# Stick-breaking attention with queries on partitions, and sixteen weight sums in another stage

## The chip, the core and the metric

The kernel runs on one core of a Trainium2 chip. The metric is the device time of one execution, in microseconds (us), the median over the runs of a kernel. The engines are TensorE (PE in the profile, its weight loads PEld), VectorE (DVE), ScalarE (ACT), GpSimd (POOL) and SyncE (SP, which here only issues DMAs).

## The reference, cut to what matters

One step of a two-layer decoder for a prompt of 1024 tokens (two groups of 512) and 8 sample tokens that share all weights. Layer 0 has a gated recurrence and attention into 256 memory tokens, layer 1 has stick-breaking attention over shared keys and values and the same memory attention; each layer ends with a SwiGLU feed-forward network (FFN, width 2816). The change touches the prompt's stick-breaking attention, 4 heads of 128:

```python
z = jnp.einsum('bqhd,bkhd->bhqk', qi, kf) * scale + bf
mask = (k_pos[None, :] < pi[:, None])[None, None]
log_keep = jnp.where(mask, jax.nn.log_sigmoid(-z), 0.0)
tail = lax.cumsum(log_keep, axis=3, reverse=True) - log_keep
w = jnp.where(mask, jnp.exp(jax.nn.log_sigmoid(z) + tail), 0.0)
return jnp.einsum('bhqk,bkhd->bqhd', w, vf)
```

With softplus(z) = -log_sigmoid(-z), the exponent of a weight is z less the sum of the softplus values of this key and of all later keys that the query may see.

## The kernel before

**Staging.** Everything is float32. Projections use fp32r products of operands that are split in a high and a low part: ScalarE casts a weight tile to fp32r (L204, L489), VectorE subtracts it from the original (L205, L490), and three products are summed. A weight tile is loaded by SP's DMA queue; five raw tiles and five split tiles are there.

**Order.** A stage is a `weave` of generators: of the streams given with a number each, the one that has done the smallest share of its number takes its next step. A planner then orders each engine's instructions by what it expects to be ready, so that matmuls of one stream stand between those of another. Each engine works its queue in that order.

**The stages that matter.** At L1517 the attention of prompt group 0 (`b0.sb`, then `b0.mem`) is woven with the first parts of the FFN of layer 0, group 1, and with 16 steps of `weight_sums(1, ...)`. At L1520 come that FFN's other parts as `ffn_w`, with the other 24 sums. At L1534 the attention of group 1 is woven with the attention of the sample tokens (`sb_sample`, `mem_sample`) and the FFN of layer 1, group 0. From L1542 `ffn_w` runs once more, for layer 1, group 1.

**`ffn_w` and the sums.** This FFN form makes gate and up with seven products in place of eight (`gate_up_w`, L471). It needs sums of blocks of the gate and up weights; `weight_sums` (L538) makes them in DRAM, for each of five parts eight DMAs on GpSimd's queue, four of which add into their target. Ahead of each DMA stands a tiny copy on GpSimd (L551) that reads a tile which the FFN has just made, and so paces the sums. For the first few columns of the first part the plain form `gate_up_q` (L442) is used. Its products go to four single PSUM banks (`Q(0)` to `Q(3)`), which lie where the pairs of banks `mmp` of the stage before were. `S()` gives one of three other banks, `B()` one of seven 128 x 512 SBUF tiles.

**The attention before (`sb_prompt`, L1303).** Keys lie on partitions. For a head and a block of 128 keys, from the last block to the first: scores of the keys against all queries that may see them (L1319), bias and clamp on VectorE (L1324), softplus on ScalarE (L1297, L1298), on the diagonal a mask (L1301), a split in high and low (L225, L226). The sum over later keys is a product: a triangle (`trir`) times the split softplus adds to the bank `rr` (L1336), VectorE subtracts `rr` from the scores (L1341), and then the triangle's complement (`cmpr`) completes the block's column sums in `rr`. ScalarE takes the exponential (L1344), and the values times the weights add to the bank `po` (L1348). `rr` and `po` hold two of the three small banks for a whole head.

**The sample attention** of the same stage gathers its cached keys and values with an indirect DMA on GpSimd's queue (L953) into one of four tiles (`C()`), and VectorE multiplies them (L912, L924).

Of the kernel before, what the change touches and what calls it, by code (L numbers as in the profile page):

```python
# [10 lines left out]
F32R = mybir.dt.float32r  # L11
I32 = mybir.dt.int32
U8 = mybir.dt.uint8
AF = mybir.ActivationFunctionType
ALU = mybir.AluOpType
# [8 lines left out]
def tile_decoder(  # L24
# [63 lines left out]
    def B(dt=F32):  # L88
        return bpool.tile([P, 512], dt, tag="b", name=nm("b"))
# [5 lines left out]
    def Q(i):  # L95
        return single[0].tile([P, 512], F32, tag=f"q{i}", name=nm("q"))
# [24 lines left out]
    def S():  # L121
        return smp.tile([P, 512], F32, tag="s", name=nm("s"))
# [49 lines left out]
    def chain(*gens):  # L172
        for g_ in gens:
            yield from g_

    def weave(*streams):

        live = [[0, n, g_] for g_, n in streams]
        while live:
            cur = min(live, key=lambda e: e[0] / e[1])  # L180
            cur[0] += 1
            try:
                next(cur[2])
            except StopIteration:
                live.remove(cur)
# [38 lines left out]
    def split_to(dst, src):  # L224
        nc.scalar.copy(dst[0], src)  # L225
        nc.vector.tensor_sub(dst[1], src, dst[0].bitcast(F32))  # L226
# [212 lines left out]
            yield  # L439
        htok.append((ht, hs_))  # L440

    def gate_up_q(l, f, xt, side, n_side):  # L442

        h, n = PW[1], NG[1]
        sg = T()
        for j in range(2):
            w = split_w(w_gu[l], 0, ND, j * DFF + f * P)
            pp = [Q(2 * j + a) for a in range(2)]
            for k in range(ND):
                wh, wl = w[k]  # L450
                for wi, (wt, xi) in enumerate(((wh, 0), (wh, 1), (wl, 0))):
                    for a in range(2):
                        ins = nc.tensor.matmul(  # L453
                            pp[a][:, :h], wt, xt[k][:, xi, a * h : (a + 1) * h],
                            start=(k == 0 and wi == 0), stop=(k == ND - 1 and wi == 2),
                        )
                c = j * ND + k + 1
                for _ in range(c * n_side // 16 - (c - 1) * n_side // 16):
                    with tc.issue_after(ins.ins):
                        next(side, None)  # L460
            for a in range(2):
                d = sg[:, a * h : (a + 1) * h]
                if j == 0:
                    act[0] = nc.scalar.activation(d, pp[a][:, :h], AF.Silu)
                else:
                    nc.vector.tensor_mul(d, d, pp[a][:, :h])
        mt = M(F32R)
        split_to((mt[:, 0, :n], mt[:, 1, :n]), sg[:, :n])
        return mt
# [93 lines left out]
    class ffn_w:  # L563
# [38 lines left out]
        def part(self, pi):  # L602
            l, n, h = self.l, NG[1], PW[1]
            f0, nf = PARTS[pi]
            last = pi == len(PARTS) - 1
            mids = []
            for j in range(nf):
                self.pi = pi
                if f0 + j < self.plain:
                    mids.append(gate_up_q(l, f0 + j, self.x, self.sums, self.steps[j]))  # L610
                    now[0] = mids[-1][:, 0, 0:1].bitcast(F32)
                else:
                    mids.append(gate_up_w(l, f0 + j, self.ops, self.spl, self.raws))
                yield
            if pi == 0:
                self.R = R_one()
            if last:
                with tc.issue_after(act[0].ins):
                    nc.scalar.preload_act_table_set("natural_log_exp_and_others")
                if self.rows:  # L620
                    yield from self.close(f0, nf, mids)
                    return
                self.acc = small([P, WID], tag="st", bufs=3)
            for m in range(ND):
                w = split_w(w_down[l], f0, nf, m * P)
                pp = [Q(2 * (m % 2) + a) for a in range(2)]
                for k in range(nf):
                    wh, wl = w[k]
                    for wi, (wt, xi) in enumerate(((wh, 0), (wh, 1), (wl, 0))):
                        for a in range(2):  # L630
                            nc.tensor.matmul(  # L631
                                pp[a][:, :h], wt, mids[k][:, xi, a * h : (a + 1) * h],
                                start=(k == 0 and wi == 0), stop=(k == nf - 1 and wi == 2),
                            )
                for a in range(2):
                    d = self.R[m][:, a * h : (a + 1) * h]
                    if pi == 0:
                        nc.scalar.copy(d, pp[a][:, :h])
                    else:
                        nc.vector.tensor_add(d, d, pp[a][:, :h])  # L640
                now[0] = self.R[m][:, 0:1]
                if last:
                    sq_acc(self.acc, self.R[m][:, :n], m, n)
                if m % 2:
                    yield
# [649 lines left out]
    def softplus(zb, e, w):  # L1295

        nc.scalar.activation(e[:, :w], zb[:, :w], AF.Exp)  # L1297
        nc.scalar.activation(e[:, :w], e[:, :w], AF.Ln, bias=1.0)  # L1298

    def keep_strict(t):  # L1300
        nc.vector.tensor_mul(t, t, sm01)  # L1301

    def sb_prompt(g, Qs, xo):  # L1303
        nkb = CH * (g + 1)
        for h in range(H):
            kh, vh = A(), A()
            nc.sync.dma_start(kh[:, : g + 1, :G], ksc[h][:, : g + 1, :])
            nc.sync.dma_start(vh[:, : g + 1, :G], vsc[h][:, : g + 1, :])
            rr = S()
            po = S()  # L1310
            nc.vector.memset(rr, 0.0)
            nc.vector.memset(po, 0.0)
            for jb in range(nkb - 1, -1, -1):
                c0 = max(0, (jb - CH * g) * P)
                w = G - c0
                diag = jb >= CH * g
                kg, kc = jb // CH, (jb % CH) * P
                ps = S()
                nc.tensor.matmul(  # L1319
                    ps[:, :w], kh[:, kg, kc : kc + P], Qs[h // 2][:, h % 2, c0:G],  # L1320
                    start=True, stop=True,
                )
                zb = B()
                nc.vector.tensor_scalar(  # L1324
                    zb[:, :w], ps[:, :w], biasp[:, h : h + 1], 44.0, op0=ALU.add, op1=ALU.min
                )
                e = B()
                softplus(zb, e, w)
                if diag:
                    keep_strict(e[:, :P])  # L1330
                hi, lo = B(F32R), B(F32R)
                split_to((hi[:, :w], lo[:, :w]), e[:, :w])

                def acc(mat):
                    for s in (hi, lo):
                        nc.tensor.matmul(  # L1336
                            rr[:, c0:], mat, s[:, :w], start=False, stop=True, skip_group_check=True
                        )

                acc(trir)  # L1340
                nc.vector.tensor_sub(zb[:, :w], zb[:, :w], rr[:, c0:])  # L1341
                if jb:
                    acc(cmpr)
                nc.scalar.activation(zb[:, :w], zb[:, :w], AF.Exp)  # L1344
                if diag:
                    keep_strict(zb[:, :P])
                vt = vh[:, kg, kc : kc + P]
                nc.tensor.matmul(po[:, c0:], vt, zb[:, :w], start=False, stop=(jb == 0), skip_group_check=True)  # L1348
                yield
            d = xo[h]  # L1350
            split_to((d[:, 0, :G], d[:, 1, :G]), po)

# [68 lines left out]
    with tc.issue_after(made[0].ins):  # L1421
# [1 line left out]
        nc.gpsimd.affine_select(  # L1423
            trif, ones, pattern=[[-1, P]], compare_op=ALU.is_ge, fill=0.0, base=0, channel_multiplier=1
        )
        trir = const.tile([P, P], F32R, name="trir")
        nc.vector.tensor_copy(trir, trif)
        cmpr = const.tile([P, P], F32R, name="cmpr")
        nc.vector.tensor_sub(cmpr, ones, trif)

        sm01 = const.tile([P, P], F32, name="sm01")
        nc.gpsimd.affine_select(
            sm01, ones, pattern=[[1, P]], compare_op=ALU.is_gt, fill=0.0, base=0, channel_multiplier=-1
        )
        sel = const.tile([P, NB, NB], F32, name="sel")
        nc.gpsimd.affine_select(
# [77 lines left out]
    b0.open()  # L1514
    f1 = ffn(1, 0, o1.x)
    ws = weight_sums(1, range(5))
    weave((chain(b0.sb(), b0.mem()), 30), (chain(f1.part(0), f1.part(1)), 18), (islice(ws, 16), 17))  # L1517
    set_banks(True)
    fw = ffn_w(0, o1.x, (5, 6, 5), 2, False, f1.R)
    weave((chain(fw.part(2), fw.part(3), fw.part(4)), 24), (ws, 24))  # L1520
    f1.acc = fw.acc
    set_banks(False)
    xk1, xb1 = [], []
# [8 lines left out]
    b1.open()  # L1532
    f0 = ffn(0, 1, o0.x)
    weave(  # L1534
        (chain(b1.sb(), b1.mem()), 40), (chain(b1.sb_sample(), b1.mem_sample()), 39),
        (chain(f0.part(0), f0.part(1), f0.part(2), f0.part(3)), 34),
    )
    o1 = out_proj(1, 1, A, True)
    drain(o1.mm(b1.xo))
# [37 lines left out]
```

## Time and profile before

| | us |
|---|---|
| median of 3 runs | 2538.38 (2535.67 to 2547.71) |
| the profiled execution | 2532.34 |
| its span | 2530.6 |
| TensorE busy | 2489.4 |
| VectorE busy | 1599.8 |
| ScalarE busy | 1208.9 |
| GpSimd busy | 116.6 |

The profile is of one execution. A line such as L1336 names the line of the kernel, then engine, operation, the tile written and the tiles read. A matmul of full fp32 operands leaves two records, one of fp32r operands and a transpose leave one. The duration of one matmul includes its way through the array; matmuls overlap, so the time that one takes from the next is less than its duration, and is read from runs of equal matmuls. Waits are given with what ended them, for instance "PE s L1336 <- ACT b L225".

### The profile page before, as it was taken

The page shows a single profiled execution, that of the slowest core. Times are in us where ns is not written, and L with a number is a line of the kernel's source. Part 1 is how long each engine was busy: PE and PEld are TensorE (multiplying, and loading weights), DVE is VectorE, ACT ScalarE, POOL GpSimd, SP SyncE. Part 2 cuts the span into 40 slices and gives each one's busy share as a digit, 9 for nine tenths or more (in the row PEclk, how much of TensorE's full clock was granted, in tenths as well). Part 3 has the DMA queues.
Part 4 walks back from the last instruction along what each step waited for, and adds up shares of the span by engine and source line. Part 5 has one row for each costly group of instructions (what it writes and reads, how often), then busy time and mean ns, then how long its engine had stood idle before and what let it go on. Part 6 is the DMA issues. An engine that isn't in the chain of part 4 may idle for free. (4 is left out here: it accounts for less than half of the span.)

```text
span 2530.6 us, 40558 instructions
## 1 busy us (share of the span) xinstructions
PE 2489.4 (98%) x15295; PEld 2158.2 (85%) x15295; DVE 1599.8 (63%) x2926; ACT 1208.9 (48%) x2321; POOL 116.6 (5%) x187
## 2 busy tenths in 40 slices
PE   8999999999999999999999999999999999999998
PEld 6888888877877888999999989876676797999998
DVE  5766556655765576655645585666577638845666
ACT  5437543333434454555434454554454445554445
POOL 1000000000000000000011200011000000000000
PEclk9999999999999999999999999999999999999999
DMA  5355656555643446576789966544444333464552
GB/s 187 114 159 126 163 170 163 136 148 144 189 125 96 129 149 206 151 183 156 192 213 271 286 179 193 159 136 123 120 139 120 96 118 117 122 191 143 151 149 74
DMA packets 521551, 391.24 MB, mean 155 GB/s; under 512 B 19973, under 2 KB 459858, under 8 KB 521354
## 3 DMA queue, kind: packets, MB, share of 16 engines
q1 hardware_dynamic: 493194, 308.94, 41.2%
q0 software_dynamic: 28160, 79.70, 13.3%
q8 instruction: 120, 1.97, 0.3%
q14 instruction: 77, 0.63, 0.1%
HBM read 358.76 MB, written 101.11 MB: 182 GB/s over the span
## 5 line engine op out<-in xcount | busy, mean ns | idle before, releaser
L218 PE MATMUL mm<-x,ws 128*128 128x512 f32 (+1 forms) x6624 | 1235.4, 341 | 2.3 <-DVE t L235 1.4
L218 PEld LDWEIGHTS mm<-x,ws 128*128 128x128 f32 x6624 | 1017.2, 188 | 167.8 <-issue 25.3
L204 ACT CAST ws<-w 128x512 fp32r<-128x512 f32 (+1 forms) x672 | 395.7, 589 | 635.9 <-PE mm L218 479.3
L205 DVE TENSOR_TENSOR ws<-w,ws 128x512 fp32r<-128x512 f32 (+1 forms) x672 | 434.8, 651 | 288.3 <-ACT ws L204 276.5
L218 PE MATMUL mm<-m,ws 128*128 128x512 f32 (+1 forms) x1536 | 345.9, 372 | 0.2 <-DVE m L226 0.2
L218 PEld LDWEIGHTS mm<-m,ws 128*128 128x128 f32 x1536 | 257.4, 189 | 55.0 <-issue 9.5
L631 PE MATMUL q<-m,ws 128*128 128x260 f32 x1440 | 180.6, 286 | 6.6 <-DVE r L640 6.6
L631 PEld LDWEIGHTS q<-m,ws 128*128 128x128 f32 x1440 | 176.6, 191 | 9.1 <-DVE r L640 3.3
L490 DVE TENSOR_TENSOR ws<-w,ws 128x512 fp32r<-128x512 f32 x164 | 112.5, 691 | 84.5 <-ACT ws L489 82.4
L489 ACT CAST ws<-w 128x512 fp32r<-128x512 f32 x164 | 101.4, 621 | 105.6 <-PE q L631 34.3
L499 PE MATMUL q<-x,ws 128*128 128x260 f32 x1008 | 134.3, 282 | 0.0
L499 PEld LDWEIGHTS q<-x,ws 128*128 128x128 f32 x1008 | 126.4, 188 | 0.0
L499 PE MATMUL q<-y,ws 128*128 128x260 f32 x912 | 119.6, 283 | 0.4 <-ACT q L506 0.2
L499 PEld LDWEIGHTS q<-y,ws 128*128 128x128 f32 x912 | 113.6, 188 | 0.9 <-ACT q L506 0.4
L235 DVE TENSOR_SCALAR t<-mm 128x512 f32<-128x512 f32 (+1 forms) x70 | 48.4, 691 | 63.0 <-PE mm L218 62.8
L453 PE MATMUL q<-x,ws 128*128 128x260 f32 x576 | 72.6, 287 | 6.4 <-DVE r L390 5.3
L695 DVE TENSOR_TENSOR t<-t,mm 128x512 f32<-128x512 f32 (+1 forms) x54 | 37.2, 689 | 65.8 <-PE mm L218 65.8
L453 PEld LDWEIGHTS q<-x,ws 128*128 128x128 f32 x576 | 70.8, 192 | 8.2 <-ACT ws L204 3.9
L390 DVE TENSOR_TENSOR r<-r,mm 128x512 f32<-128x512 f32 (+1 forms) x72 | 49.4, 686 | 32.8 <-PE mm L218 31.9
L239 DVE TENSOR_TENSOR t<-t,t 128x512 f32<-128x512 f32 (+1 forms) x54 | 37.4, 692 | 51.4 <-ACT t L238 51.4
L226 DVE TENSOR_TENSOR m<-t,m 128x512 fp32r<-128x512 f32 (+1 forms) x88 | 60.9, 692 | 6.2 <-ACT m L225 5.1
L258 DVE TENSOR_TENSOR st<-st,n 128x512 f32<-128x512 f32 (+1 forms) x91 | 62.3, 691 | 3.4 <-ACT n L257 1.9
(343 smaller groups left out, 2859.3 us busy)
## 6 DMA issues: line engine op xcount, KB each, us to landing
w<-in_w_gu SPq DMA_DIRECT2D x310, 256.0 KB, 3.1
w<-in_w_down SPq DMA_DIRECT2D x160, 256.0 KB, 2.9
wsum<-in_w_gu POOLq DMA_DIRECT2D x36, 1024.0 KB, 9.5
w<-wsum SPq DMA_DIRECT2D x94, 256.0 KB, 3.2
w<-in_w_in_a SPq DMA_DIRECT2D x80, 256.0 KB, 3.1
w<-in_w_o SPq DMA_DIRECT2D x64, 256.0 KB, 2.9
wsum<-in_w_gu POOLq DMA_DIRECT2D x12, 1280.0 KB, 10.5
wsum<-wsum POOLq DMA_DIRECT2D x12, 1024.0 KB, 6.3
```

Of the source, the lines that this page charges most:

```text
L204: nc.scalar.copy(ws[:, 0, :n, :], raw[:, :n, :])
L205: nc.vector.tensor_sub(ws[:, 1, :n, :], raw[:, :n, :], ws[:, 0, :n, :].bitcast(F32))
L218: nc.tensor.matmul(ps[:, a, : PW[g]], wt, xt[k][:, xi, o : o + PW[g]], start=(k == 0 and wi == 0), stop=(k == nk - 1 and wi == 2),)
L226: nc.vector.tensor_sub(dst[1], src, dst[0].bitcast(F32))
L235: nc.vector.tensor_scalar(sv(x, g), pv(ps, g), -44.0, None, op0=ALU.max)
L258: nc.vector.tensor_add(acc[:, :n], acc[:, :n], t[:, :n])
L390: nc.vector.tensor_add(dst, dst, pv(ps, g))
L453: ins = nc.tensor.matmul(pp[a][:, :h], wt, xt[k][:, xi, a * h : (a + 1) * h], start=(k == 0 and wi == 0), stop=(k == ND - 1 and wi == 2),)
L489: nc.scalar.copy(w[:, 0, :], src)
L490: nc.vector.tensor_sub(w[:, 1, :], src, w[:, 0, :].bitcast(F32))
L499: nc.tensor.matmul(ps[:, :h], w[:, wj, k * P : (k + 1) * P], x[:, xi, :], start=(first and k == 0 and wi == 0), stop=(k == 3 and wi == 2), ...
L631: nc.tensor.matmul(pp[a][:, :h], wt, mids[k][:, xi, a * h : (a + 1) * h], start=(k == 0 and wi == 0), stop=(k == nf - 1 and wi == 2),)
```

## The change

Queries now lie on partitions and keys along the row. A unit is a block of 128 queries (`c`) against the keys of one group (`s`): its own group up to the diagonal (128 to 512 keys) or the whole earlier group (512). The first two widths of blocks 0 and 2 share a unit. The sum over later keys is a scan along the reversed row, `tensor_tensor_scan` with add, started for the earlier group from the last value of the later one. The weights are then transposed in blocks of 128 by TensorE, copied to SBUF by ScalarE, and multiplied with the values block by block. These last steps of a unit are issued after the first steps of the next unit. `trir`, `cmpr` and `rr` go, and the mask `sm01` is transposed.

Sixteen of the weight sums move from the weave at L1520 to that at L1534. The first product of the first plain `ffn_w` column goes to banks from `S()`. Three weave numbers change.

```diff
--- before.py
+++ after.py
@@ -439,13 +439,13 @@
             yield
         htok.append((ht, hs_))
 
-    def gate_up_q(l, f, xt, side, n_side):
+    def gate_up_q(l, f, xt, side, n_side, first):
 
         h, n = PW[1], NG[1]
         sg = T()
         for j in range(2):
             w = split_w(w_gu[l], 0, ND, j * DFF + f * P)
-            pp = [Q(2 * j + a) for a in range(2)]
+            pp = [Q(2 * j + a) if j or f != first else S() for a in range(2)]
             for k in range(ND):
                 wh, wl = w[k]
                 for wi, (wt, xi) in enumerate(((wh, 0), (wh, 1), (wl, 0))):
@@ -607,7 +607,7 @@
             for j in range(nf):
                 self.pi = pi
                 if f0 + j < self.plain:
-                    mids.append(gate_up_q(l, f0 + j, self.x, self.sums, self.steps[j]))
+                    mids.append(gate_up_q(l, f0 + j, self.x, self.sums, self.steps[j], PARTS[self.first][0]))
                     now[0] = mids[-1][:, 0, 0:1].bitcast(F32)
                 else:
                     mids.append(gate_up_w(l, f0 + j, self.ops, self.spl, self.raws))
@@ -1301,52 +1301,64 @@
         nc.vector.tensor_mul(t, t, sm01)
 
     def sb_prompt(g, Qs, xo):
-        nkb = CH * (g + 1)
+
+        units = [[(0, g), (2, g)], [(1, g)], [(3, g)]]
+        if g:
+            units = [u for c in ((0, 2), (1,), (3,)) for u in ([(i, 1) for i in c], *([(i, 0)] for i in c))]
+
+        def weights(h, kh, unit, first):
+            ps, spans, o = S(), [], 0
+            for c, s in unit:
+                w = (c + 1) * P if s == g else G
+                spans.append((c, s, o, w))
+                nc.tensor.matmul(
+                    ps[:, o : o + w], Qs[h // 2][:, h % 2, c * P : (c + 1) * P], kh[:, s, :w], start=True, stop=True
+                )
+                o += w
+            zb = B()
+            nc.vector.tensor_scalar(zb[:, :o], ps[:, :o], biasp[:, h : h + 1], 44.0, op0=ALU.add, op1=ALU.min)
+            e = B()
+            softplus(zb, e, o)
+            for c, s, a, w in spans:
+                if s == g:
+                    keep_strict(e[:, a + w - P : a + w])
+                d = e[:, a : a + w][:, ::-1]
+                nc.vector.tensor_tensor_scan(d, d, d, first.get(c, 0.0), op0=ALU.add, op1=ALU.max)
+                first[c] = e[:, a : a + 1]
+            nc.vector.tensor_sub(zb[:, :o], zb[:, :o], e[:, :o])
+            nc.scalar.activation(zb[:, :o], zb[:, :o], AF.Exp)
+            for c, s, a, w in spans:
+                if s == g:
+                    keep_strict(zb[:, a + w - P : a + w])
+            return zb, spans, o
+
+        def values(vh, po, zb, spans, n):
+            pt = S()
+            for o in range(0, n, P):
+                nc.tensor.transpose(pt[:, o : o + P], zb[:, o : o + P], ident)
+            wt = B()
+            nc.scalar.copy(wt[:, :n], pt[:, :n])
+            for c, s, a, w in spans:
+                for o in range(0, w, P):
+                    nc.tensor.matmul(
+                        po[:, c * P : (c + 1) * P], vh[:, s, o : o + P], wt[:, a + o : a + o + P],
+                        start=False, stop=(s == 0 and o == w - P), skip_group_check=True,
+                    )
+
         for h in range(H):
             kh, vh = A(), A()
             nc.sync.dma_start(kh[:, : g + 1, :G], ksc[h][:, : g + 1, :])
             nc.sync.dma_start(vh[:, : g + 1, :G], vsc[h][:, : g + 1, :])
-            rr = S()
             po = S()
-            nc.vector.memset(rr, 0.0)
             nc.vector.memset(po, 0.0)
-            for jb in range(nkb - 1, -1, -1):
-                c0 = max(0, (jb - CH * g) * P)
-                w = G - c0
-                diag = jb >= CH * g
-                kg, kc = jb // CH, (jb % CH) * P
-                ps = S()
-                nc.tensor.matmul(
-                    ps[:, :w], kh[:, kg, kc : kc + P], Qs[h // 2][:, h % 2, c0:G],
-                    start=True, stop=True,
-                )
-                zb = B()
-                nc.vector.tensor_scalar(
-                    zb[:, :w], ps[:, :w], biasp[:, h : h + 1], 44.0, op0=ALU.add, op1=ALU.min
-                )
-                e = B()
-                softplus(zb, e, w)
-                if diag:
-                    keep_strict(e[:, :P])
-                hi, lo = B(F32R), B(F32R)
-                split_to((hi[:, :w], lo[:, :w]), e[:, :w])
-
-                def acc(mat):
-                    for s in (hi, lo):
-                        nc.tensor.matmul(
-                            rr[:, c0:], mat, s[:, :w], start=False, stop=True, skip_group_check=True
-                        )
-
-                acc(trir)
-                nc.vector.tensor_sub(zb[:, :w], zb[:, :w], rr[:, c0:])
-                if jb:
-                    acc(cmpr)
-                nc.scalar.activation(zb[:, :w], zb[:, :w], AF.Exp)
-                if diag:
-                    keep_strict(zb[:, :P])
-                vt = vh[:, kg, kc : kc + P]
-                nc.tensor.matmul(po[:, c0:], vt, zb[:, :w], start=False, stop=(jb == 0), skip_group_check=True)
+            first, late = {}, None
+            for unit in units:
+                now_ = weights(h, kh, unit, first)
+                if late:
+                    values(vh, po, *late)
+                late = now_
                 yield
+            values(vh, po, *late)
             d = xo[h]
             split_to((d[:, 0, :G], d[:, 1, :G]), po)
 
@@ -1423,14 +1435,10 @@
         nc.gpsimd.affine_select(
             trif, ones, pattern=[[-1, P]], compare_op=ALU.is_ge, fill=0.0, base=0, channel_multiplier=1
         )
-        trir = const.tile([P, P], F32R, name="trir")
-        nc.vector.tensor_copy(trir, trif)
-        cmpr = const.tile([P, P], F32R, name="cmpr")
-        nc.vector.tensor_sub(cmpr, ones, trif)
 
         sm01 = const.tile([P, P], F32, name="sm01")
         nc.gpsimd.affine_select(
-            sm01, ones, pattern=[[1, P]], compare_op=ALU.is_gt, fill=0.0, base=0, channel_multiplier=-1
+            sm01, ones, pattern=[[-1, P]], compare_op=ALU.is_gt, fill=0.0, base=0, channel_multiplier=1
         )
         sel = const.tile([P, NB, NB], F32, name="sel")
         nc.gpsimd.affine_select(
@@ -1514,10 +1522,10 @@
     b0.open()
     f1 = ffn(1, 0, o1.x)
     ws = weight_sums(1, range(5))
-    weave((chain(b0.sb(), b0.mem()), 30), (chain(f1.part(0), f1.part(1)), 18), (islice(ws, 16), 17))
+    weave((chain(b0.sb(), b0.mem()), 25), (chain(f1.part(0), f1.part(1)), 18), (islice(ws, 16), 17))
     set_banks(True)
     fw = ffn_w(0, o1.x, (5, 6, 5), 2, False, f1.R)
-    weave((chain(fw.part(2), fw.part(3), fw.part(4)), 24), (ws, 24))
+    weave((chain(fw.part(2), fw.part(3), fw.part(4)), 24), (islice(ws, 8), 8))
     f1.acc = fw.acc
     set_banks(False)
     xk1, xb1 = [], []
@@ -1532,8 +1540,8 @@
     b1.open()
     f0 = ffn(0, 1, o0.x)
     weave(
-        (chain(b1.sb(), b1.mem()), 40), (chain(b1.sb_sample(), b1.mem_sample()), 39),
-        (chain(f0.part(0), f0.part(1), f0.part(2), f0.part(3)), 34),
+        (chain(b1.sb(), b1.mem()), 45), (chain(b1.sb_sample(), b1.mem_sample()), 39),
+        (chain(f0.part(0), f0.part(1), f0.part(2), f0.part(3)), 34), (ws, 17),
     )
     o1 = out_proj(1, 1, A, True)
     drain(o1.mm(b1.xo))
```

## The prediction

> **What bounds the kernel now.** I read the page first, then the busy time by stage, then TensorE's waits in each stage, then the DMA of the stages that lose time. The page's busy time by engine (us, share of the span, instructions):
>
> ```profile
> PE 2489.4 (98%) x15295; PEld 2158.2 (85%) x15295; DVE 1599.8 (63%) x2926; ACT 1208.9 (48%) x2321; POOL 116.6 (5%) x187
> ```
>
> TensorE is busy 98% of the span, so a matmul that goes is time that goes, unless a wait takes its place. Busy time is a share over the whole span, so the stages come next (columns: stretch, its length, busy time of each engine, granted clock, DMA share, GB/s).
>
> ```profile
> 915.00:1225.00 310.00, 309.82 (x2003) 275.47 (x2002) 187.25 (x347) 158.46 (x308) 15.36 (x28) 1.00 0.61 167
> 1225.00:1475.00 250.00, 238.72 (x1879) 233.28 (x1879) 144.35 (x286) 108.88 (x216) 40.95 (x60) 0.98 0.95 249
> 1600.00:2040.00 440.00, 434.55 (x1842) 317.04 (x1841) 292.76 (x485) 208.98 (x401) 25.43 (x24) 1.00 0.42 125
> 2150.00:2400.00 250.00, 247.49 (x2040) 244.20 (x2041) 157.60 (x310) 129.86 (x274) 0.00 (x0) 1.00 0.52 150
> ```
>
> These are the attention of group 0 (line 1517), the first Strassen FFN (line 1520), the attention of group 1 (lines 1534 to 1537), and most of the last FFN. TensorE idles 0.2, 11.3, 5.5 and 2.5 us in them. The two FFN stages do the same kind of work; the one that loses 11.3 us has the DMA engines 95% busy, the other 52%. TensorE's waits (us in total, times, longest) in the second, third and fourth stage:
>
> ```profile
> PE q L631 <- DVE r L640: 6.6, 5, 1.9
> PE q L453 <- DVE r L390: 3.7, 1, 3.7
> PE s L1336 <- ACT b L225: 2.1, 1, 2.1
> PE s L1336 <- DVE b L226: 1.9, 2, 1.0
> PE s L1348 <- DVE b L1301: 0.5, 2, 0.3
> PE q L453 <- DVE r L390: 1.5, 1, 1.5
> ```
>
> In the FFN, matmuls wait for VectorE to empty a bank (L640, L390). What keeps VectorE is seen from ScalarE's waits in that stage, and from the DMA rows (queue: packets, MB, share; transfers: count, KB, us to landing) there and, last two, in 2150 to 2400:
>
> ```profile
> ACT ws L489 <- DMA w<-wsum: 14.5, 3, 5.5
> ACT ws L204 <- DMA w<-in_w_down: 6.7, 1, 6.7
> q0 software_dynamic: 10924, 29.78, 48.9%
> w<-in_w_down SPq DMA_DIRECT2D x26, 256.0 KB, 5.7
> w<-wsum SPq DMA_DIRECT2D x18, 256.0 KB, 5.7
> w<-wsum SPq DMA_DIRECT2D x59, 256.0 KB, 3.2
> w<-in_w_down SPq DMA_DIRECT2D x24, 256.0 KB, 2.9
> ```
>
> So weights land late (5.7 us against about 3), ScalarE's cast of them waits, VectorE's split waits for the cast, and the evacuation queued behind the split holds TensorE. Half of the DMA engines' time there is GpSimd's queue, which is the weight sums. Each longer wait costs more than itself:
>
> ```profile
> 1254.30:1257.70 3.40, 2.93 (x13) 2.96 (x14) 2.21 (x5) 1.01 (x3) 0.00 (x0) 0.50 1.01 294
> ...
> 1715.10:1718.50 3.40, 3.40 (x10) 2.67 (x9) 2.67 (x8) 2.23 (x6) 1.96 (x2) 0.50 0.29 85
> ```
>
> These are the first and the last of four such rows (the others start at 1315.70 and 1452.30): after a wait the granted clock is 0.50 for 3.4 us, so 1.7 us are lost each time, three times in the FFN and once in group 1's attention.
>
> Here the Trainium skill ("TensorE: Matmul & The Clock Gate", section "HAM oscillation — how this bites in real kernels") speaks against counting all four: it asks for an idle gap of over about 3.4 us. By it one halving (after 3.7 us) hangs on these waits, and the sum below would gain 5.1 us less. The trace disagrees: the clock halved after waits of 1.9 and 2.1 us too.
>
> **The change part by part.** *Matmuls of the attention.* Gone are both products with the triangle and its complement (L1336). Rows: the two groups; then runs from the timeline (start, us), from which a price is the run less one duration, or the difference of two runs.
>
> ```profile
> L1336 PE MATMUL s<-b,trir x96: 222/394/800, 1028.4 to 1954.6; 128*128 128x512 f32 x48, 128*128 128x128 f32 x16, 128*128 128x256 f32 x16, 128*128 128x384 f32 x16
> L1336 PE MATMUL s<-b,cmpr x80: 222/342/825, 1029.5 to 1939.7; 128*128 128x512 f32 x32, 128*128 128x128 f32 x16, 128*128 128x256 f32 x16, 128*128 128x384 f32 x16
> 2135.64 13.31 PE L218 MATMUL mm<-m,ws 128*128 128x512 f32 x57
> 2037.34 22.84 PE L218 MATMUL mm<-x,ws 128*128 128x260 f32 x186
> L1319 PE MATMUL s<-a,a 128*128 128x512 f32 x48 | 25.1, 605 | 0.2 <-DVE b L1324 0.2
> 1769.66 1.02 PE L1319 MATMUL s<-a,a 128*128 128x512 f32 x2
> 83.97 1.06 PE L1130 MATMUL s<-a,a 128*128 128x128 f32 x8
> 85.30 1.95 PE L1130 MATMUL s<-a,a 128*128 128x128 f32 x16
> 2505.78 1.03 PE L732 MATMUL s<-ident,r 128*128 128x128 f32 x8
> 2520.01 1.47 PE L732 MATMUL s<-ident,r 128*128 128x128 f32 x12
> L218 PEld LDWEIGHTS mm<-x,ws 128*128 128x128 f32 x6624 | 1017.2, 188 | 167.8 <-issue 25.3
> ```
>
> An fp32r pass costs 13.31/57 = 234 ns at 512 columns and 22.84/186, about 122, at 260; 384 columns I put at 175 between them, 256 at 118, 128 at the 111 of the next price. Gone: 80 x 0.234 + 32 x (0.175 + 0.118 + 0.111) = 31.6 us. A full fp32 product is two records; one costs 1.02 - 0.605 = 0.42 us at 512 columns, 0.89/8 = 111 ns at 128, between them 0.32 at 384 and 0.21 at 256. A transpose is one record of 0.44/4 = 110 ns.
>
> Scores keep their columns (1280 a head in group 0, 3328 in group 1; only the operands swap roles): nothing. The weighted values were 48 x 0.42 + 16 x (0.32 + 0.21 + 0.11) = 30.4 us and become 36 blocks x 4 heads x 2 = 288 records of 128 columns, 32.0 us: +1.6. New are 144 transposes: +15.8. Net -31.6 + 1.6 + 15.8 = **-14.2 us**. The bound on the other side is the weight load, 188 ns by the last row if nothing hid it (a rival).
>
> Here the Trainium skill ("TensorE: Matmul & The Clock Gate", section "Back-to-back issue gap") gives about 81 ns a matmul at 128 columns with its weight load. By it the 432 new records would cost 13 us less than I count. The trace has 110 and 111, and I stay with it.
>
> *VectorE and ScalarE.* Rows by shape (count | busy, mean ns | idle before):
>
> ```profile
> L226 DVE TENSOR_TENSOR b<-b,b 128x512 fp32r<-128x512 f32 x24 | 16.6, 690 | 15.4 <-ACT b L225 15.4
> L1160 DVE COPY_PREDICATED b<-mask,s 128x256 f32<-128x256 uint8 x56 | 25.8, 527 | 0.0
> ```
>
> The split's subtraction goes; the scan comes over the same 18432 columns. No scan is in this trace. Bounds: a subtraction's 1.35 ns a column (25 us in all) and the dearest row a column, 2.06 ns (38 us); I take the upper end, as a scan feeds each result into the next. VectorE is free 123 us in the first attention stage and 147 in the second, so it costs nothing; without that cover it would cost the 13 us difference. Masks stay 64; the cast to hi is replaced by the copy of the transposed weights, of the same width. The clearing of rr and two constants go: nothing, VectorE isn't late there. Nor do the new shares of the weave: the attention keeps its pace in group 0 (20 steps at 25 for 24 at 30) and ends earlier in group 1, with FFN steps left to fill TensorE.
>
> *Waits in the chain.* Two of the three places where TensorE stood in an attention step go: the 4.0 us before L1336, also the 0.5 before L1348 and one halving of 1.7: 6.2. What is late next: transposes behind the exponential (one step later in the program, so a step of FFN matmuls lies between) and values behind ScalarE's copy. The memory attention has this very pattern, and its waits in 1600 to 2040 were:
>
> ```profile
> PE s L885 <- ACT b L883: 0.3, 1, 0.3
> ```
>
> In 40 units (3 a head in group 0, 7 in group 1) that is little; bounds 0 and 28 us (0.69 us each, a pass over 512 columns by L226's row).
>
> *Sixteen sums moved* out of the FFN at 1225. All that they issue goes with them: a mark on GpSimd and a transfer each of 512 x 512 x 4 bytes, 16 of that queue's 29.8 MB. That takes 0.49 x 16/29.8 = 0.26 off the DMA share, to 0.69. SP's queue, which loads the weights, keeps its transfers. The stage should then resemble its twin: of 11.3 us of idling and 5.1 of halved clock, 16.4 in all, I keep 3.4 (its twin's 2.5 and something for the eight sums left): **-13.0**. Bounds 0 and 16.4. They now run beside group 1's attention, where DMA goes from 0.42 to 0.42 + 0.26 x 250/440 = 0.57; at 0.61 the stage from 915 lost 0.2 us. Their first use is in the last FFN (line 1542). But GpSimd's queue also holds that stage's page gathers, and those have little cover:
>
> ```profile
> 1771.11 0.95 POOL L953 DMA_INDIRECT c<-in_cache_sb_v,pidx  x1 [0.30 <-issue]
> 1774.75 1.23 DVE L924 TENSOR_TENSOR c<-c,sc 128x1024 f32<-128x1024 f32 x1 [1.26 <-DMA c<-in_cache_sb_v,pidx]
> c<-in_cache_sb_v,pidx POOLq DMA_INDIRECT x16, 4.1
> c<-in_cache_sb_k,pidx POOLq DMA_INDIRECT x8, 10.1
> 1282.67 0.64 POOL L551 COPY mk<-m 128x1 f32<-128x1 f32 x1 [12.10 <-ACT m L225]
> ```
>
> VectorE already waited 1.3 us for a gather; beside the sums of 1225 to 1475 gathers landed in 10.1 us instead of 4.1, and a mark holds the queue until an FFN step is done (12.1 us here). Queued behind the waiting gather are VectorE's weight splits, and TensorE waits for these once the five buffers of split weights are used. I charge 3.8: the stage's waits net **-2.4** (6.2 - 3.8).
>
> *First bank of the FFN* taken from the small pool: the 1.5 us at 2150 go, **-1.5**; the 3.7 at 1254 are in the 13.0, since the weights were late there too.
>
> Sum: 14.2 + 13.0 + 2.4 + 1.5 = 31.1 us. The profiled execution took 2532.3 us (span 2530.6), so it becomes 2501.2. The median of the runs shown is 6.0 above that execution; I carry that over: **2507 us**, with 2494 to 2520 as this case's own range.
>
> **The rivals.** *The FFN keeps its stalls* (the change doesn't do what it says: its own weight loads, not the sums, fill the DMA). For it: eight sums stay. Against: the twin stage. Gives 2507 + 13 = 2520. *Weight loads bind the small passes*: 432 x 0.188 - 31.6 - 30.4 = +19.2 instead of -14.2, so 2540; against it the 111 ns of whole runs. *Values wait for the copies* at every unit: +28, 2535; against it the pattern's one wait of 0.3. *Slower: gathers behind sums.* In 1700 to 1780 eight tiles of cached values each come 6.0 us later (10.1 - 4.1), VectorE's queue stands, TensorE runs out of weights, and a halving of 1.7 follows: 8 x 7.7 = 62, 2569. It decides from 5.5 us lost a tile. For it: the 1.3 us already seen. Against: split weights lie ready, and sums are spread over 440 us. Two smaller cases lie within the forecast's own range and share its chance: the clock halves as often as now although waits go (4 x 1.7 back, 2514; 0.05), and small passes cost less than the 110 ns that every run of them shows (each 10 ns is 4.3 us; at 81 ns 2494; 0.03).
>
> **How the numbers follow.** Forecast 0.62, FFN stalls stay 0.12, copies 0.11, weight loads 0.05, gathers 0.07, others 0.03. About 0.5% (12.7 us) is what a measurement can tell from no change. Faster than 2525.7: the first two and a third of the others, 0.75. Within: copies, loads and a third of the others, 0.17. Slower: gathers and the rest, 0.08. The range goes down to 2492: every wait gone (3.4 + 3.8 less) gives 2500, without the 6.0 carried over 2494, and a little for the prices read from runs. It goes up to 2536, which takes in the stalls that stay and the copies. Loads, gathers, the others beyond it and the forecast's own tails are the 0.2 left out.
>
> **What would show it.** Per step: no L1336, 144 transposes at about 110 ns and 288 value passes at 111; 1225 to 1475 with DMA near 0.69, weights landing in under 4 us, no L631 wait over 1 us and no halved clock; the scan under 2.1 ns a column and VectorE under 75% in the attention; gathers landing in under 6 us there, and no VectorE wait on them over 3 us. Wrong if TensorE idles over 8 us in either attention stage, or if the FFN still waits on L640.

## The result and the profile after

| | us |
|---|---|
| before, median of 4 runs | 2537.03 (2531.45 to 2547.71) |
| changed, median of 4 runs | 2514.22 (2512.76 to 2514.93) |
| ratio of the medians, 95% interval | 0.9909 [0.989, 0.9928] |
| profiled execution, before and after | 2532.34 and 2513.78 |

The kernel is 23 us faster, where 30 were forecast. One term of the sum, group 1's attention, went the other way, and the stages show it. TensorE's busy time on the page of the changed kernel, then its stages (stretch, length, busy time of each engine, granted clock, DMA share, GB/s); group 1's attention starts 18 us earlier than before:

```profile
PE 2467.7 (98%) x15455; PEld 2160.5 (86%) x15455; DVE 1609.2 (64%) x2900; ACT 1197.4 (48%) x2289; POOL 119.6 (5%) x187
```

```profile
915.00:1225.00 310.00, 308.62 (x2071) 277.61 (x2070) 194.01 (x350) 158.83 (x303) 15.18 (x28) 1.00 0.62 168
1225.00:1470.00 245.00, 241.90 (x1900) 236.12 (x1900) 153.05 (x293) 114.03 (x221) 25.15 (x28) 0.99 0.71 195
1590.00:2030.00 440.00, 422.24 (x1960) 323.02 (x1959) 297.88 (x470) 199.97 (x384) 45.09 (x56) 0.98 0.57 160
2130.00:2400.00 270.00, 267.39 (x2203) 263.95 (x2201) 172.45 (x336) 144.12 (x301) 0.00 (x0) 1.00 0.53 152
```

The FFN idles 3.1 us instead of 11.3, with DMA at 0.71. Group 1's attention idles 17.8 us instead of 5.5, with DMA at 0.57 instead of 0.42. What TensorE waits for there, and VectorE's waits for DMA in the same stretch (us in total, times, longest):

```profile
PE s L1343 <- ACT b L1340: 5.1, 2, 3.9
PE s L1338 <- DVE b L1301: 5.0, 3, 4.5
PE s L878 <- DVE b L871: 4.4, 2, 2.5
PE s L1314 <- DVE b L1319: 2.5, 1, 2.5
```

```profile
DVE c L912 <- DMA b<-qd: 13.8, 9, 3.2
DVE c L924 <- DMA c<-in_cache_sb_v,pidx: 12.0, 2, 8.1
DVE c L924 <- DMA c<-in_cache_mem_v: 8.1, 5, 3.6
```

The waits stand at many lines, but the second list is one story: VectorE stands still 33.9 us for data of the sample attention (`qd` is the broadcast of the sample queries); before, these three rows were

```profile
DVE c L912 <- DMA b<-qd: 7.0, 5, 2.3
DVE c L924 <- DMA c<-in_cache_sb_v,pidx: 2.3, 3, 1.3
DVE c L924 <- DMA c<-in_cache_mem_v: 2.2, 2, 2.0
```

One case in order of time, from the timelines of GpSimd, VectorE and TensorE (start, duration, line, idle before):

```profile
1744.15 0.97 POOL L953 DMA_INDIRECT c<-in_cache_sb_v,pidx  x1 [17.20 <-PE ns L926]
1745.46 1.14 POOL L554 DMA_DIRECT2D wsum<-in_w_gu  x1
1746.90 1.05 POOL L953 DMA_INDIRECT c<-in_cache_sb_v,pidx  x1 [0.31 <-issue]
1756.42 1.23 DVE L924 TENSOR_TENSOR c<-c,sc 128x1024 f32<-128x1024 f32 x1 [8.11 <-DMA c<-in_cache_sb_v,pidx]
1762.69 1.09 PE L1338 MATMUL s<-ident,b 128*128 128x128 f32 x4 [4.47 <-DVE b L1301]
```

A tile of cached values comes in two gathers, and a sum of 1 MB was issued between them. The first gather landed in 4.0 us, the second in 9.4:

```profile
c<-in_cache_sb_v,pidx POOLq DMA_INDIRECT x1, 4.0
c<-in_cache_sb_v,pidx POOLq DMA_INDIRECT x1, 9.4
```

VectorE waits 8.1 us for the second one, the masks and scans queued behind come late, and TensorE stands 4.5 us at a transpose. Most gathers were not late: the median of the 16 is 4.6 us to landing, 4.1 before, and VectorE's 12.0 us are two waits, both for a gather issued behind a sum. Followed back in the same way on the timelines, TensorE's waits of 2.5, 4.5 and 1.2 us (at 1727, 1763 and 1768) stand behind these two gathers, and those of 3.9, 2.5 and 2.0 (at 1698, 1921 and 1930) behind the broadcast of the sample queries: about half of the 17.8 us each.

The clock is halved in three stretches of this stage instead of one, the first of twice the length; each begins within 1.3 us of the end of one of these waits (3.9, 2.5 and 4.5 us):

```profile
1697.40:1704.20 6.80, 6.46 (x22) 5.77 (x23) 4.61 (x11) 1.75 (x7) 0.95 (x1) 0.51 0.52 156
1728.10:1731.50 3.40, 3.40 (x14) 3.04 (x14) 3.33 (x5) 2.14 (x4) 0.00 (x0) 0.51 0.89 282
1762.20:1765.70 3.50, 3.01 (x7) 1.01 (x8) 2.48 (x7) 2.50 (x5) 0.00 (x0) 0.52 0.46 129
```

### The profile page after: what moved, and what is told of

The parts are those of the page before. It is cut to its first block, busy times and chain, and to the rows that moved or that the text cites. A ratio compares the mean times of both kernels' runs of the same rounds, so it can differ in the third digit from the quotient of the medians.

```text
span 2511.9 us, 40889 instructions
## 1 busy us (share of the span) xinstructions
PE 2467.7 (98%) x15455; PEld 2160.5 (86%) x15455; DVE 1609.2 (64%) x2900; ACT 1197.4 (48%) x2289; POOL 119.6 (5%) x187
## 4 chain that ended last, share of the span: by engine, by line
PE 90%; DVE 4%; DMA 3%; ACT 1%; issue 1%; SPq 0%; POOL 0%; DVEq 0%; ACTq 0%
PE mm L218 53%; PE q L499 11%; PE q L631 7%; PE q L453 2%; PE s L1150 2%; PE mm L1018 2%; DMA b<-qd 1%; PE s L1343 1%; PE s L885 1%; PE s L854 1%; PE mm L803 1%; PE mm L830 1%; PE s L1314 1%; PE q L663 1%; PE ns L926 1%
## 5 line engine op out<-in xcount | busy, mean ns | idle before, releaser
L218 PE MATMUL mm<-x,ws 128*128 128x512 f32 (+1 forms) x6624 | 1216.0, 340 | 2.4 <-DVE t L235 1.5
L218 PEld LDWEIGHTS mm<-x,ws 128*128 128x128 f32 x6624 | 1013.6, 189 | 155.5 <-issue 17.4
L218 PE MATMUL mm<-m,ws 128*128 128x512 f32 (+1 forms) x1536 | 329.3, 367 | 0.0
L499 PE MATMUL q<-x,ws 128*128 128x260 f32 x1008 | 134.3, 282 | 0.0
L499 PEld LDWEIGHTS q<-x,ws 128*128 128x128 f32 x1008 | 126.4, 188 | 0.0
L225 ACT CAST m<-t 128x512 fp32r<-128x512 f32 (+1 forms) x88 | 54.9, 624 | 21.7 <-DVE t L695 13.0
L453 PE MATMUL q<-x,ws 128*128 128x260 f32 x480 | 61.0, 288 | 3.7 <-DVE r L390 2.2
```

What stands on the lines that cost most here:

```text
L218: nc.tensor.matmul(ps[:, a, : PW[g]], wt, xt[k][:, xi, o : o + PW[g]], start=(k == 0 and wi == 0), stop=(k == nk - 1 and wi == 2),)
L453: ins = nc.tensor.matmul(pp[a][:, :h], wt, xt[k][:, xi, a * h : (a + 1) * h], start=(k == 0 and wi == 0), stop=(k == ND - 1 and wi == 2),)
L499: nc.tensor.matmul(ps[:, :h], w[:, wj, k * P : (k + 1) * P], x[:, xi, :], start=(first and k == 0 and wi == 0), stop=(k == 3 and wi == 2), ...
```

## The experiments

Two theories were set against each other. Late transfers: loads of the sample attention that share the DMA engines with the moved sums stop VectorE. The attention itself: the longer scan, and copies queued behind softplus on ScalarE, make the waits. The first four kernels:

**Sums back in the FFN** (`e1_sums_back`)

```diff
-    weave((chain(fw.part(2), fw.part(3), fw.part(4)), 24), (islice(ws, 8), 8))
+    weave((chain(fw.part(2), fw.part(3), fw.part(4)), 24), (ws, 24))
...
-        (chain(f0.part(0), f0.part(1), f0.part(2), f0.part(3)), 34), (ws, 17),
+        (chain(f0.part(0), f0.part(1), f0.part(2), f0.part(3)), 34),
```

> The changed kernel with the sixteen sums back in the FFN stage (line 1525 of the changed kernel), all else as changed. Late-transfer theory (gathers and loads queued beside the sums stop VectorE in group 1's attention): TensorE idles under 6 us in 1590 to 2030 (17.8 with the change), VectorE waits for cached values under 4 us in total (12.0), while the FFN stage idles about 11 us again with its clock halved two or three times; 2514 - 17 + 13 = about 2510 us. Attention theory (the new form itself, its longer scan and the copies queued behind ScalarE's softplus, makes the waits): the stage still idles 14 us or more, and the FFN's loss comes on top: about 2527 us.

Measured: 2514.8 us, ratio 0.9918 [0.9902, 0.9935]. Its FFN stage and group 1's attention:

```profile
1225.00:1470.00 245.00, 231.67 (x1824) 227.19 (x1824) 135.87 (x266) 103.96 (x204) 43.83 (x60) 0.97 0.95 249
1590.00:2030.00 440.00, 434.05 (x2097) 336.39 (x2097) 310.41 (x489) 208.49 (x397) 25.71 (x24) 1.00 0.42 127
```

The attention idles 6.0 us in place of 17.8 (5.5 before), the FFN 13.3 in place of 3.1. So the new attention by itself idles no more than the old one, and in the changed kernel the move of the sums paid nothing: what the FFN gained, the attention lost. The time is nearer to the 2510 of the late-transfer theory than to 2527. Its bound for cached values was too low: VectorE still waits 5.4 us for them, not under 4.

**The move alone, on the kernel before** (`e2_move_only`)

```diff
-    weave((chain(fw.part(2), fw.part(3), fw.part(4)), 24), (ws, 24))
+    weave((chain(fw.part(2), fw.part(3), fw.part(4)), 24), (islice(ws, 8), 8))
...
-        (chain(f0.part(0), f0.part(1), f0.part(2), f0.part(3)), 34),
+        (chain(f0.part(0), f0.part(1), f0.part(2), f0.part(3)), 34), (ws, 17),
```

> The kernel before with the sixteen sums moved to group 1's attention and nothing else changed. Late-transfer theory: the FFN stage gains about 11 us, group 1's attention loses 12 to 18 (it idled 5.5 us): 2532 to 2538 us, no gain. Attention theory: the FFN's gain remains, the old attention still idles about 5.5 us: about 2521 us.

Measured: 2545.4 us, ratio 1.0034 [1.0023, 1.0046]: 9 us slower, more than either theory said. Group 1's attention idles 21.7 us (5.5 before), the FFN 4.7 (11.3 before). The stage, TensorE's longest waits there, then one wait of VectorE for the broadcast and TensorE's wait behind it, from the timeline:

```profile
1600.00:2040.00 440.00, 418.29 (x1667) 299.48 (x1666) 281.81 (x468) 199.15 (x380) 46.38 (x56) 0.98 0.56 154
PE s L1336 <- ACT b L225: 14.9, 3, 6.9
```

```profile
1707.49 1.23 DVE L912 TENSOR_TENSOR c<-c,b 128x1024 f32<-128x1024 f32 x1 [7.07 <-DMA b<-qd]
1709.41 0.58 PE L1336 MATMUL s<-b,trir 128*128 128x256 f32 x1 [6.95 <-ACT b L225]
```

The broadcast comes through SP's queue, not GpSimd's, so the queue of gathers is not the only way in which the sums hurt. The old attention stands up to 7 us where VectorE stands. Its products with the triangle wait for the split on ScalarE and VectorE in the middle of each step; that this makes it lose more than the new form is argued, not shown.

**The FFN's first bank as before** (`e3_old_bank`)

```diff
-            pp = [Q(2 * j + a) if j or f != first else S() for a in range(2)]
+            pp = [Q(2 * j + a) for a in range(2)]
```

> The changed kernel with the first FFN product back in the bank that the stage before empties. If the small pool's bank was worth what the prediction said: the wait of L453 for L390 comes back at the last FFN (1.5 us) and grows at the first (2.2 us to about 3.7), so 2 to 3 us more than the changed kernel, 2517. If the weights were late anyway: within 1 us of it.

Measured: 2519.1 us, ratio 0.9929 [0.9912, 0.9945]. The two waits in its FFN stages, then the one in the changed kernel:

```profile
PE q L453 <- DVE r L390: 7.4, 1, 7.4
PE q L453 <- DVE r L390: 1.5, 1, 1.5
```

```profile
PE q L453 <- DVE r L390: 2.2, 1, 2.2
```

By the waits the bank is worth the 1.5 us in the last FFN and 5.2 in the first, more than the forecast gave it. The two kernels differ by 4.8 us, but the intervals of their ratios still overlap a little (0.9912 against 0.9928).

**Sums beside an earlier stage** (`e4_sums_early`)

```diff
-    weave((chain(a1.merge(), a1.mem()), 12), (a1.mem_sample(), 20), (chain(f0.part(2), f0.part(3)), 16))
+    early = weight_sums(1, range(3, 5))
+    weave(
+        (chain(a1.merge(), a1.mem()), 12), (a1.mem_sample(), 20), (chain(f0.part(2), f0.part(3)), 16), (early, 17),
+    )
...
-    ws = weight_sums(1, range(5))
+    ws = weight_sums(1, range(3))
```

and the weave of group 1's attention has no sums.

> The changed kernel with the sixteen sums in the weave of 700 to 850 us (DMA share 0.36, no page gathers) instead of group 1's attention. Late-transfer theory: the FFN keeps its gain and group 1's attention idles under 6 us: 2514 - 17 = about 2497 us. Attention theory: 2511 to 2515 us.

Measured: 2499.8 us, ratio 0.9863 [0.9847, 0.9879], faster than both kernels. The stage that took the sums, the FFN and group 1's attention:

```profile
700.00:850.00 150.00, 147.81 (x632) 110.63 (x631) 89.00 (x150) 59.07 (x120) 14.75 (x22) 1.00 0.72 192
1225.00:1470.00 245.00, 241.35 (x1909) 235.41 (x1908) 153.24 (x295) 114.03 (x223) 25.16 (x28) 1.00 0.72 196
1590.00:2030.00 440.00, 434.80 (x2115) 337.25 (x2114) 304.23 (x480) 207.25 (x396) 26.25 (x24) 1.00 0.42 127
```

The FFN keeps its gain (3.7 us of idling), the attention idles 5.2 us, and the stage that took the sums loses 2.2. The late-transfer theory stands; the time is 3 us above its 2497. VectorE's waits for cached values are 5.8 us here, which is what the stage has without any sums. What this left open: the marks or the transfers, the gathers' queue or the shared DMA engines, and whether VectorE had room at all.

**Sums in the second half of group 1's attention** (`e5_sums_late`; `pause(n, g)` yields n times, then runs `g`)

```diff
-        (chain(f0.part(0), f0.part(1), f0.part(2), f0.part(3)), 34), (ws, 17),
+        (chain(f0.part(0), f0.part(1), f0.part(2), f0.part(3)), 34), (pause(18, ws), 35),
```

> The changed kernel with the sixteen sums still in group 1's attention, but held back until half of the FFN steps there are done, after the last gather of cached values. Queue theory (what hurts are page gathers behind a sum in GpSimd's queue): VectorE's 12 us of waits for cached values go, the stage idles about 8 us, 2503 us. Bandwidth theory (any load that shares the DMA engines with a 1 MB sum lands late, also SP's broadcasts of the sample queries and its loads of the memory's values): the waits move to these, the stage idles 12 us or more, 2508 us or more.

Measured: 2502.1 us, ratio 0.9876 [0.9858, 0.9894]. VectorE's waits for DMA in the stage:

```profile
DVE c L917 <- DMA b<-qd: 8.8, 8, 3.6
DVE c L929 <- DMA c<-in_cache_mem_v: 5.8, 3, 3.1
DVE c L929 <- DMA c<-in_cache_sb_v,pidx: 4.8, 4, 2.6
```

Cached values are waited for 4.8 us instead of 12.0, the others still 14.6 (8.5 with the early sums). The stage idles 7.8 us (432.24 busy of 440), as the queue theory said. So most of the loss came from sums in the half with the gathers. The waits that SP's loads still cause cost TensorE 2.9 us in the second half. The run doesn't part the two causes: in the half that is now free of sums the broadcasts come nearer to their time too (2.5 us of waits up to 1740, 7.7 in the changed kernel).

**Marks alone** (`e7_marks_only`): the early sums, and in group 1's attention a stream of 16 copies as of L551, without a DMA.

> The kernel with the early sums, plus sixteen marks alone (the tiny copies on GpSimd that wait for the FFN) in group 1's attention, without transfers. If it is the marks that hold the gathers in GpSimd's queue: VectorE waits 10 us or more for cached values again, 2507 or more. If it is the transfers: within 2 us of the kernel with the early sums, 2498 to 2502.

Measured: 2501.3 us, ratio 0.987 [0.9849, 0.9891]; the stage idles 6.0 us (434.00 of 440), the waits for cached values are 6.1 us, against 5.8 without marks. Not the marks: the transfers.

**Every scan twice** (`e6_scan_twice`, on the early sums)

```diff
                 nc.vector.tensor_tensor_scan(d, d, d, first.get(c, 0.0), op0=ALU.add, op1=ALU.max)
+                nc.vector.tensor_tensor_scan(d, d, d, first.get(c, 0.0), op0=ALU.max, op1=ALU.max)
```

> The kernel with the early sums, with every scan followed by a second one of the same length in place (a running maximum, which changes nothing), so that VectorE does some 45 us more in the two attention stages and each chain is up to 1.3 us longer. If VectorE has room, as the prediction said: within 4 us of the kernel with the early sums, 2500 to 2504. If VectorE's queue is close to setting the pace (FFN splits behind scans): 8 us or more on top, 2508 and up.

Measured: 2509.3 us, ratio 0.9898 [0.9877, 0.9919], 9.5 us more than the kernel with the early sums, and over the 4 us that free room on VectorE allows (the two intervals just overlap, 0.9877 against 0.9879). The second scan's groups (count | busy, mean ns), and TensorE's waits in group 1's attention:

```profile
L1327 DVE TENSOR_TENSOR_SCAN b<-b 128x128 f32<-128x128 f32 (+3 forms) x32 | 25.3, 810 | 0.3
L1327 DVE TENSOR_TENSOR_SCAN b<-b,b 128x512 f32<-128x512 f32 x16 | 20.5, 1281 | 0.4
```

```profile
PE s L1339 <- DVE b L1301: 4.5, 3, 2.4
PE s L1339 <- ACT b L1330: 4.2, 6, 1.0
```

46 us more on VectorE cost about a fifth of that. VectorE's idle time covers most of such work, not all, so "it costs nothing" in the prediction was too strong.

**No sums in the FFN** (`e8_ffn_free`): the early sums, with the eight that were left in the FFN ahead of group 0's attention (the weaves at L1508 and L1509 of the kernel before).

> The kernel with the early sums, with the eight sums that were left in the FFN stage moved to the weaves before group 0's attention, so that the FFN stage has none. It idled 3.7 us in the kernel with the early sums. If its own loads suffice to keep it, nothing is gained (2499); if the eight sums make it, 2 to 3 us go, 2497; if the new place loses as much as the old one gains, 2500 or more.

Measured: 2511.1 us, ratio 0.9911 [0.9891, 0.9931], 11 us worse: the new place loses more than the old one gains, the third case of the forecast. The FFN idles 3.2 us (241.80 of 245), as with eight sums, and the stretch from 915 to 1225 now 6.2 (303.78 of 310), most of it one wait of 4.8 at 923, with the clock halved for 6.8 us around it. Ahead of it ScalarE waited for two late weight tiles of the output projection:

```profile
PE ns L247 <- DVE st L258: 4.8, 1, 4.8
ACT ws L204 <- DMA w<-in_w_o: 6.8, 2, 4.7
```

The 4.9 us of idling that came with it and the 3.4 lost to the clock are 8 of the 11 us.

**Half of the triangle's passes** (`e9_no_lo`, on the kernel before; the low part of the softplus is left out of the sums)

```diff
-                    for s in (hi, lo):
+                    for s in (hi,):
```

> The kernel before, in which the running sums take only the high part of the split softplus: the low part is made but not multiplied, so 88 of the 176 passes of L1336 are left out (and the sums are less exact). By the run prices that is half of 31.6, 15.8 us: 2536 - 16 = 2520. If each of these passes, standing alone between others and waiting for its operand, cost more than its price in a run (the attention stages hold some 7 us more than prices, idling and halved clock explain): 20 us or more, 2516 or less. If removing the passes only uncovers the chain's waits: 10 us or less, 2526 or more.

Measured: 2518.4 us, ratio 0.9927 [0.9911, 0.9943], that is 14 to 23 us less. The run prices (15.8) fit; whether a lone pass costs more is open.

## Why the prediction was right, and where it was wrong

The time lies in the forecast's own range, and the direction and two of the gains, the matmuls and the FFN, were as worked out. One step failed in both of its parts, and the prediction's own sign of being wrong, TensorE idling over 8 us in an attention stage, came true (17.8). Two lucky turns, told below, hide part of that in the time. Against the profiled execution of before, which was 18.6 us longer where 31.1 were forecast:

- **Matmuls, -14.2.** Right in its counts (144 transposes, 288 value passes, no L1336) and prices. The two groups after, then runs of the timeline:

```profile
L1338 PE MATMUL s<-ident,b 128*128 128x128 f32 x144 | 24.1, 281 | 7.0 <-DVE b L1301 6.2 <-ACT b L1329 0.6
L1343 PE MATMUL s<-b,a 128*128 128x128 f32 x288 | 43.1, 293 | 5.1 <-ACT b L1340 5.1
1605.99 0.60 PE L1338 MATMUL s<-ident,b 128*128 128x128 f32 x4
1653.32 1.07 PE L1343 MATMUL s<-b,a 128*128 128x128 f32 x8
```

  Eight value passes take 1.07 us where eight of L1130 took 1.06; four transposes 0.60, less a duration of 0.28 by its group about 110 ns each. So the weight load of 188 ns stays hidden. The 81 ns of the Trainium skill ("TensorE: Matmul & The Clock Gate", section "Back-to-back issue gap") does not hold for these float32 passes either.
- **Sums out of the FFN, -13.0.** Right: idling fell by 8.2 us and one halving was left of three (-3.4), so -11.6; from the kernel with the sums back to that with the early sums the time fell 15 us. The DMA share was forecast at 0.69 and was 0.71. One small wait for L640 was left, 0.9 us.
- **Group 1's attention, -2.4.** This step failed. The stage came to +17.4 (idling +12.3, halved clock +5.1).

  Its first part, 6.2 us of waits and halved clock that go with L1336, hardly came. Without sums in the stage, the kernel with the sums back idles 6.0 us there with one halved stretch, as much as before (5.5 and one); the kernel with the early sums idles 5.2 with none, 2.0 us better. The old waits went, but the transposes now wait, which the step had called little. From the kernel with the early sums:

```profile
PE s L1338 <- DVE b L1301: 3.1, 2, 2.9
PE s L1338 <- ACT b L1329: 1.1, 3, 0.5
```

  Its second part, the 3.8 us charged for late gathers, was far too small: the sums' share was about 12 us of idling and the halvings after it. This is what the rival "gathers behind sums" describes, but at about 1.5 us of idling for each of the eight tiles, below its point of decision of 5.5. The step also left out SP's loads: the broadcast stopped VectorE 13.8 us (7.0 before), and about half of TensorE's idling hangs on it. The inference from DMA share, that 0.57 would do because 0.61 did from 915 to 1225, was the wrong one. A likely reason, not tested alone, is that in that stage VectorE waited directly for a load only once, 2.5 us.
- **First bank, -1.5.** The 1.5 in the last FFN went. At the first it was worth more than the late weights suggested: a wait of 7.4 us without it (`e3_old_bank`), 2.2 with it.
- **The scan, nothing.** Its price was above the bound taken: 45.9 us in all (25.4 and 20.5), not 38. By the doubled scan about a fifth of extra VectorE time reaches the end, so the 15 us over the subtraction and clearing that went (30.6 by the rows of before) are some 3 us, an estimate.

These terms give -14.2 - 11.6 + 17.4 and about -1 for the last FFN, -9.4 of 18.6. Two small losses come on top: 1.2 us more of idling in group 0's attention, and one more halved stretch at 608 (1.7), in a part that the change doesn't touch. So the other 9 us, 12 with these two, lie between the matmuls: TensorE's busy time fell by 21.7 us, more than the passes account for, although the clock was halved for longer. Counting each record of a stage at its run price and taking off idling and halved clock, an estimate, 2.6 us less is left over in group 0's attention than before and 5.1 in group 1's. That passes waiting for an operand cost more than in a run would explain it; `e9_no_lo` could not tell, and it stays open.

That gain was forecast by no term, and is the first piece of luck. Without the move (`e1_sums_back`) the kernel is 21.6 us faster than before, and the forecast's terms for the rest give 14.2 + 6.2 + 1.5 = 21.9; but the 6.2 didn't come, and the unexplained gain stands in their place. The second is the 6.0 us carried over from execution to median. They did not recur: the changed kernel's median is 0.4 above its profiled execution. So the time came out 7 us from the forecast, while the steps were 12.5 off.

## What to carry to other kernels

A transfer that nobody waits for can still delay the loads beside it: before choosing its new stage by the DMA share, look for the loads that an in-order engine waits for directly, and with how much lead they are issued. Replacing products on the bound engine by a scan on another pays about what the passes cost in a run, here 14 us by their prices, as long as the other engine has idle time in that very stage. When a change has several parts, run each alone: here the new attention, with the bank and the weave numbers, gave all of the gain, and the moved sums nothing until their target stage was changed. The weave numbers were not tried alone.

## What the runs showed of the hardware

A scan over 512 float32 columns took VectorE 1.22 to 1.28 us, against 0.69 for a subtraction of the same width. The Trainium skill ("DVE: opcode table, instruction layouts, handler registers and perf-mode slots", section "Datapath and trigger behaviour") says that the built-in scan runs at half throughput, and the trace comes near it: 0.54 to 0.56 of the subtraction's rate.

```profile
L1326 DVE TENSOR_TENSOR_SCAN b<-b,b 128x512 f32<-128x512 f32 x16 | 20.5, 1280 | 9.6 <-ACT b L1298 9.6
L1326 DVE TENSOR_TENSOR_SCAN b<-b 128x512 f32<-128x512 f32 x8 | 9.8, 1224 | 0.2
```

The same sixteen sums cost 2 us of TensorE's idling beside one stage, 12 beside another and 10 beside a third, at DMA shares of 0.72, 0.57 and 0.95: the share did not order the losses.

In group 1's attention of the changed kernel, the two waits of 4.4 us together at L878 (the longest 2.5) were followed by no halved clock, while in the kernel before a wait of 1.9 was. The length of a wait alone does not decide it.
